# The MLP of the last 1224 tokens by seven products of halves instead of eight, in two halves of tokens

## The chip, the cores and the metric

The kernel runs on one core of one Trainium2 chip. Its engines are TensorE (PE; PEld is its weight load), VectorE (DVE), ScalarE (ACT), GpSimd (POOL) and SyncE (SP, which issues the transfers). The metric is the device time of one execution in microseconds (us), lower is better.

## The reference, cut to what matters

One decoder layer over 2048 prompt tokens and 8 new tokens, 2056 in all, with 1024 features. The part that changes is the MLP, all in float32:

```python
def _mlp(h, g, w_up, w_down):          # w_up (1024, 4096), w_down (4096, 1024)
    a = jax.nn.relu(rmsnorm(h, g) @ w_up)
    return (a * a) @ w_down
...
hp = hp + _mixer_out(outs, lses, pooled, w_out[i])
hp = hp + _mlp(hp, norm_mlp_g[i], w_up[i], w_down[i])
hp = hp + _ple(hp, p_prompt[i], ple_norm_g[i], w_ple_gate[i], w_ple[i])
```

`_ple` is a gate, `(p @ w_ple) * sigmoid(rmsnorm(h) @ w_ple_gate)`; a last RMSNorm follows.

## The kernel before

Activations lie transposed, features on the 128 partitions and tokens in the columns. Every float32 operand of a product is kept as two parts, the value rounded to fp32r and the rest of it, and a product is three matmuls (`PASSES`: high by high, high by low, low by high), so that one 128x128 weight tile by one chunk of tokens costs three matmuls into one bank of PSUM. `load_w` loads a weight tile, makes its high part on POOL (`pcopy`, L199) and its low part on DVE (a subtraction by `tt`, L196).

From the MLP on, the tokens go in two parts: X, the first 832 (chunks `CX`, two of 416), and Y, the last 1224 (chunks `CY`: 416, 416 and 392). In time: input projection and attention; MLP of X (attention of the later heads runs beside it); output projection of Y; gate of X; MLP of Y (about 1720 to 2570 us); gate of Y with the final norm. The change is in the MLP of Y, called MLP-Y below, and in what stands at its borders.

`mlp` walks 4096 hidden features in 8 blocks of 512. A block has an up side (four groups j of 128 hidden features, 24 matmuls a chunk, then relu on ACT at L1344, square on POOL, the high part on ACT at L1347, the low part on DVE) and a down side (8 output tiles `ft` times 3 chunks, 12 matmuls each, added from PSUM to the accumulator `hacc` by DVE). MLP-Y has 8 x (4 x 3 x 24 + 8 x 3 x 12) = 4608 matmuls. Each weight is loaded once for the 1224 tokens.

The program is written in the order above with generators that lay other work beside it (`Pace`, `hook`); a scheduler then sets the order on each engine, and each engine runs its own queue in that order, waiting on semaphores. `R` and `F` are two regions of on-chip memory for operands in two parts (`mem_r`) and plain float32 (`mem_f`; `mem_ma` and `mem_mb` are pieces that pass from one to the other). `tt(eng, out, a, b, op)` is an element-wise operation of two tensors on DVE (`V`) or POOL (`G`).

Of the kernel before, what the change touches and what calls it, by code (L numbers as in the profile page):

```python
# [17 lines left out]
P = 128  # L18
# [19 lines left out]
CY = [(2 * LC, LC), (3 * LC, LC), (4 * LC, T - 4 * LC)]  # L38
NX, NY = 2 * LC, T - 2 * LC

# [8 lines left out]
class Arena:  # L49
# [15 lines left out]
    def alloc(self, cols, keys=None, high=False):  # L65
# [7 lines left out]
        s = max(fits, key=lambda s: s[1]) if high else min(fits, key=lambda s: (s[3], s[2]))  # L73
# [75 lines left out]
def decoder_step(ctx: ExitStack, tc: tile.TileContext, I, O):  # L149
# [103 lines left out]
    qkvS = DR([3, NS, H * E], "qkvs_s")  # L253
    s0S = DR([2, NS * H], "s0_s")
# [97 lines left out]
    class Acts:  # L352
# [824 lines left out]
    class Stat:  # L1177


        def __init__(self, chunks, tp, eng=V):  # L1180
# [4 lines left out]
            self.sq = Ring(F, 2, LC)  # L1185
# [8 lines left out]
        def finish(self, ci):  # L1194
            ln, a, ps = self.chunks[ci][1], self.acc[ci], self.tp()
            q = ln // 4
            for i in range(4):
                mm(ps[:q, i : i + 1], a[:, i * q : i * q + q], ones[:, :1], True, True)
            v, s1, s2, r = (TINY(4, q, key="st", n=8, width=4) for _ in range(4))
            V.tensor_scalar(v, ps[:q, :4], 1.0 / D, EPS, op0=ALU.mult, op1=ALU.add)  # L1200
            newton(r, v, s1, s2)
            ps = self.tp()
            for i in range(4):
# [185 lines left out]

    def load_acc(src, chunks):  # L1390
# [6 lines left out]
    def gate(xa, hacc, sums, cis, getw, hook, step=None):  # L1397


        base, s0 = xa.chunks[0][0], xa.chunks[cis[0]][0]  # L1400
        sr, pr = Ring(F, 2, LC), Ring(F, 2, LC)
        for ft in range(KD):
            w = getw(ft)
            for ci in cis:
# [11 lines left out]
                hc = hacc[ft].ap[:, c0 - base : c0 - base + ln]  # L1416
# [7 lines left out]
                else:  # L1424
                    S.activation(hc, hc, AF.Copy, scale=g_fin[:, ft : ft + 1])
                if step:
                    step(ft, s)
# [6 lines left out]
    class Final:  # L1434


        def __init__(self, hacc, base, sums, p0, p1):
            self.hacc, self.base, self.sums, self.p0, self.tiles = hacc, base, sums, p0, []
# [5 lines left out]
        def add_up(self, ps, src, start, stop):  # L1444
            order = range(len(self.tiles))
            for i in order if start(0) else reversed(order):
# [17 lines left out]
        def turn(self, i, ft, ps):  # L1464
            p, rw = self.tiles[i]
            PE.transpose(ps[:rw, (ft % 4) * P : (ft % 4) * P + P], self.hacc[ft].ap[:, p - self.base : p - self.base + rw], ident)  # L1466
# [14 lines left out]
    def final(hacc, base, sums, p0, p1, yr):  # L1481
        fin, ps = Final(hacc, base, sums, p0, p1), tp()
# [164 lines left out]
    for b in (rr, xg):  # L1647
        b.free()
# [59 lines left out]
```

## Time and profile before

| what | value |
|---|---|
| time, median of 2 runs | 2735.38 us (2733.13 to 2737.62) |
| the profiled execution: its time, its span | 2732.91 us, 2731.2 us |
| mean granted TensorE clock, in parts of full speed | 0.991 |
| PE busy | 2651.1 us, 97% |
| DVE, POOL, ACT busy | 1559.9, 1030.2, 846.6 us (57, 38, 31%) |

The span runs from the first instruction to the last. Busy shares are means over stages with different limits, so the stage of MLP-Y has to be read by itself. A line number can be that of a helper: L190 is every matmul, L196 every element-wise operation of two tensors, and the tiles and shapes tell which is meant.

### The profile page before, as it was taken

The page shows a single profiled execution, that of the slowest core. Times are in us where ns is not written, and L with a number is a line of the kernel's source. Part 1 is how long each engine was busy: PE and PEld are TensorE (multiplying, and loading weights), DVE is VectorE, ACT ScalarE, POOL GpSimd, SP SyncE. Part 2 cuts the span into 40 slices and gives each one's busy share as a digit, 9 for nine tenths or more (in the row PEclk, how much of TensorE's full clock was granted, in tenths as well). Part 3 has the DMA queues.
Part 4 walks back from the last instruction along what each step waited for, and adds up shares of the span by engine and source line. Part 5 has one row for each costly group of instructions (what it writes and reads, how often), then busy time and mean ns, then how long its engine had stood idle before and what let it go on. Part 6 is the DMA issues. An engine that isn't in the chain of part 4 may idle for free. (4 is left out here: it accounts for less than half of the span.)

```text
span 2731.2 us, 43094 instructions
## 1 busy us (share of the span) xinstructions
PE 2651.1 (97%) x15686; PEld 2526.3 (92%) x15686; DVE 1559.9 (57%) x3373; ACT 846.6 (31%) x1605; POOL 1030.2 (38%) x1370
## 2 busy tenths in 40 slices
PE   8999999998999999999999898999999999999998
PEld 6888899978988999999999898999999999999997
DVE  6747867675587776775765857432332332332675
ACT  6221445463434134243343424301001011011354
POOL 2415745434385444343344626312112122122263
PEclk9999999999999999999999999999999999999999
DMA  7464345476154233342322545331111111111134
GB/s 248 133 180 124 86 121 136 110 224 177 49 150 113 81 88 82 97 107 71 99 73 66 167 142 149 127 104 39 42 41 42 39 39 39 39 39 39 53 84 150
DMA packets 386194, 272.51 MB, mean 100 GB/s; under 512 B 91722, under 2 KB 349461, under 8 KB 385973
## 3 DMA queue, kind: packets, MB, share of 16 engines
q1 hardware_dynamic: 385397, 269.68, 34.6%
q8 instruction: 123, 2.02, 0.3%
q14 instruction: 90, 0.74, 0.1%
q0 software_dynamic: 512, 0.07, 0.0%
q10 hardware_dynamic: 72, 0.02, 0.0%
HBM read 209.47 MB, written 60.30 MB: 99 GB/s over the span
## 5 line engine op out<-in xcount | busy, mean ns | idle before, releaser
L190 PE MATMUL bank<-mem_r 128*128 128x416 f32 (+11 forms) x13608 | 2454.0, 338 | 46.9 <-DVE mem_r L196 13.3
L190 PEld LDWEIGHTS bank<-mem_r 128*128 128x128 f32 (+2 forms) x13608 | 2307.9, 184 | 127.4 <-DVE mem_r L196 22.9
L199 POOL TENSOR_SCALAR mem_r<-mem_f 128x512 fp32r<-128x512 f32 (+1 forms) x444 | 325.2, 737 | 773.6 <-PE bank L190 689.1
L196 DVE TENSOR_TENSOR mem_r<-mem_f,mem_r 128x512 fp32r<-128x512 f32 (+3 forms) x568 | 435.5, 773 | 176.2 <-POOL mem_r L199 142.8
L196 DVE TENSOR_TENSOR mem_f<-bank,mem_f 128x416 f32<-128x416 f32 (+3 forms) x488 | 272.7, 566 | 234.5 <-PE bank L190 227.6
L196 DVE TENSOR_TENSOR mem_r<-mem_mb,mem_r 128x416 fp32r<-128x416 f32 (+6 forms) x236 | 174.0, 744 | 349.3 <-ACT mem_r L1347 318.3
L1344 ACT ACTIVATE mem_mb<-bank 128x392 f32<-128x392 f32 (+1 forms) x160 | 82.2, 514 | 801.0 <-PE bank L190 801.0
L196 POOL TENSOR_TENSOR mem_mb<-mem_mb 128x416 f32<-128x416 f32 (+1 forms) x140 | 143.7, 1027 | 304.2 <-ACT mem_mb L1344 277.9
L776 DVE CUSTOM_DVE_ANT_0 bank<-bank,mask 128x256 f32<-128x256 f32 (+3 forms) x504 | 159.8, 338 | 33.9 <-PE bank L190 30.1
L199 POOL TENSOR_SCALAR mem_r<-mem_r 128x256 fp32r<-128x256 f32 (+1 forms) x117 | 92.0, 798 | 92.2 <-PE bank L190 81.1
L196 DVE TENSOR_TENSOR mem_ma<-bank,mem_ma 128x416 f32<-128x416 f32 (+2 forms) x104 | 63.4, 610 | 87.5 <-PE bank L190 72.8
L1347 ACT CAST mem_r<-mem_mb 128x416 fp32r<-128x416 f32 (+1 forms) x128 | 68.5, 535 | 134.4 <-POOL mem_mb L196 134.4
L859 POOL TENSOR_SCALAR_AFFINE_SELECT mem_ma<-mem_ma 128x256 f32<-128x256 f32 (+2 forms) x148 | 72.0, 506 | 92.2 <-ACT mem_ma L871 49.3
L190 PE MATMUL bank<-mem_mb,mem_r 128*64 128x64 f32 (+4 forms) x494 | 100.7, 321 | 6.2 <-DVE mem_r L196 2.1
L190 PEld LDWEIGHTS bank<-mem_mb,mem_r 128*128 128x128 f32 (+1 forms) x494 | 78.7, 174 | 16.0 <-POOL mem_r L199 2.8
L196 DVE TENSOR_TENSOR mem_r<-mem_ma,mem_r 128x512 fp32r<-128x512 f32 (+4 forms) x88 | 71.6, 819 | 26.4 <-ACT mem_r L880 20.5
L199 POOL TENSOR_SCALAR mem_r<-mem_mb 128x512 fp32r<-128x512 f32 (+3 forms) x61 | 55.3, 913 | 79.4 <-PE bank L190 55.8
L196 POOL TENSOR_TENSOR mem_f<-mem_f 128x416 f32<-128x416 f32 (+2 forms) x52 | 70.0, 1351 | 31.3 <-DMA mem_f<-in_cache_attn_kv_dram 11.4
L776 DVE DVE_READ_ACCUMULATOR2_ANT mem_ma<- 128x1 f32 (+1 forms) x512 | 68.5, 134 | 0.0
L196 POOL TENSOR_TENSOR mem_ma<-mem_ma 128x416 f32<-128x416 f32 (+1 forms) x41 | 51.8, 1272 | 39.7 <-DMA mem_ma<-h_s 14.1
L196 DVE TENSOR_TENSOR mem_f<-mem_f,mem_ma 128x416 f32<-128x416 f32 (+1 forms) x64 | 46.9, 733 | 26.2 <-ACT mem_ma L1190 11.3
L859 POOL TENSOR_SCALAR_AFFINE_SELECT mem_mb<-mem_mb 128x256 f32<-128x256 f32 (+2 forms) x76 | 34.5, 474 | 57.9 <-ACT mem_mb L868 22.8
(255 smaller groups left out, 1807.7 us busy)
## 6 DMA issues: line engine op xcount, KB each, us to landing
mem_f<-in_w_up_dram SPq DMA_DIRECT2D x128, 256.0 KB
mem_f<-in_w_down_dram SPq DMA_DIRECT2D x128, 256.0 KB
mem_f<-in_w_in_dram SPq DMA_DIRECT2D x64, 256.0 KB
out_dram<-mem_f SPq DMA_DIRECT2D x55, 256.0 KB
mem_f<-in_cache_attn_kv_dram SPq DMA_DIRECT2D x48, 256.0 KB
mem_f<-in_w_ple_gate_dram SPq DMA_DIRECT2D x48, 256.0 KB
mem_f<-in_x_prompt_dram SPq DMA_DIRECT2D x64, 128.0 KB
xT_s<-mem_f SPq DMA_DIRECT2D x32, 256.0 KB
```

The source lines that it names most:

```text
L190: PE.matmul(out, l, r, start=start, stop=stop)
L196: eng.tensor_tensor(out, a, b, op=op)
L199: G.tensor_scalar(out, src, 1.0, 1.0, op0=ALU.mult, op1=ALU.mult)
L776: V.tensor_tensor_reduce(src, src, mask, 1.0, -3e38, ALU.add, ALU.max, mcol[: src.shape[0], col : col + 1])
L859: G.affine_select(out=p, in_=p, pattern=[[0, nblk], [sign, w]], compare_op=ALU.is_ge, fill=0.0, base=base, channel_multiplier=-sign)
L1344: S.activation(a, ps[:, :ln], AF.Relu)
L1347: S.copy(x[:, 0], sq)
```

## The change

MLP-Y works in two halves of 612 tokens, each two chunks of 306 (`HY`; `CY` is now four chunks of 306). In each half, tokens, inner features and outer features of a product are split in two, and the 2x2 block product is made of seven products instead of eight (`SEVEN`, Winograd's form of Strassen's), each of half size. For that, sums of blocks are formed ahead: of the weights by four additions or subtractions of 256 columns on POOL (`w_sums`), of the activations by four of 306 columns (`z_sums`). A weight of four blocks becomes seven slots: four as loaded (1024 columns) and three sums (768 columns); an activation becomes seven slots of 306 columns. All seven are split into high part (ACT) and low part (DVE), in `parts` and `z_parts`. The products meet in three banks (`b` 0, 1, 2), which are read out after certain products (`p`) and go on accumulating.

A block of 512 hidden features in a half has four steps of 84 matmuls: two up steps (j = 0, 1) and two down steps (o = 0, 2). `Fill` prepares the weights of one step (two `Weights7`) while the step before runs. Both halves load and prepare all weights. X's hidden state goes through DRAM (`hxS`) and its final norm is made from there; the first half of Y goes through `h2`.

```diff
-CY = [(2 * LC, LC), (3 * LC, LC), (4 * LC, T - 4 * LC)]
+HY = NY // 4
+CY = [(NX + i * HY, HY) for i in range(4)]
...
+    SEVEN = ((0, 0, 0, 1), (3, 3, 2, 5), (1, 1, 1, 2), (5, 5, 0, 6), (6, 2, 2, 3), (4, 4, 0, 7), (2, 6, 0, 4))
+    OPENS = (1, 2, 5)
+    def w_sums(raw, s):
+        tt(G, s[:, 0], raw[:, 0], raw[:, 3], ALU.subtract)
+        tt(G, raw[:, 3], raw[:, 3], raw[:, 2], ALU.add)
+        tt(G, s[:, 1], raw[:, 3], raw[:, 0], ALU.subtract)
+        tt(G, s[:, 2], raw[:, 1], s[:, 1], ALU.subtract)
+    def z_sums(z, eng):
+        tt(eng[0], z[:, 4], z[:, 2], z[:, 3], ALU.subtract)
+        tt(eng[1], z[:, 3], z[:, 3], z[:, 0], ALU.subtract)
+        tt(eng[2], z[:, 5], z[:, 2], z[:, 3], ALU.subtract)
+        tt(eng[3], z[:, 6], z[:, 1], z[:, 5], ALU.subtract)
+    def z_parts(dst, z):
+        for a, b in ((0, 3), (3, 7)):
+            S.copy(dst[:, 0, a:b], z[:, a:b])
+            tt(V, dst[:, 1, a:b], z[:, a:b], f(dst[:, 0, a:b]), ALU.subtract)
...
+        def parts(self, three):
+            src, ring = (self.b, self.w3) if three else (self.a, self.w4)
+            w = [x.rearrange("p (s n) -> p s n", s=3 if three else 4) for x in ring()]
+            S.copy(w[0], src)
+            tt(V, w[1], src, f(w[0]), ALU.subtract)
...
+    def prep_seven(src, rs, gc, xs, pair, zr):
...
+            for t in range(2):
+                zt = z[:, 2 * t : 2 * t + 2]
+                tt(G, zt, zt, rb[t].ap.unsqueeze(1).to_broadcast([P, 2, ln]), ALU.mult)
...
+            z_sums(z, (V, V, V, V))
...
+            z_parts(z_parts_view(x.ap), z)
...
+    def mlp_seven(xs, get_acc, rings, zr, fill, before_last, done):
+        ln = HY
+        bsets = [[bank[0], bank[1], bank[3]], [bank[4], bank[5], bank[6]]]
...
+                for slot_w, slot_z, b, p in SEVEN:
+                    products(bs, slot_w, slot_z, b, p, ws, x)
+                    ps = bs[b][:, :ln]
+                    if p in (1, 5, 6, 4):
+                        S.copy(z[:, {1: 0, 5: 2, 6: 3, 4: 1}[p]], ps)
+                    else:
+                        i = {2: 0, 3: 3, 7: 2}[p]
+                        tt(V, z[:, i], ps, z[:, i], ALU.add)
+                    if p == 7:
+                        fill.late()
+                S.activation(z[:, 0:4], z[:, 0:4], AF.Relu)
+                tt(G, z[:, 0:4], z[:, 0:4], z[:, 0:4], ALU.mult)
+                z_sums(z, (G, G, V, V))
+                r = R.alloc(14 * ln, ("r",))
+                rl.append(r)
+                z_parts(z_parts_view(r.ap), z)
...
+            for o in (0, 2):
+                pair = fill.take()
+                for slot_w, slot_z, b, p in SEVEN:
+                    for u in range(2):
+                        bs = bsets[u]
+                        products(bs, slot_w, slot_z, b, p, [pair[u]], zs)
...
+                        if p == 2 or p == 4:
+                            t = zr[1](ln)
+                            S.copy(t, bs[b][:, :ln])
+                            tt(G, hc, hc, t, ALU.add)
+                        else:
+                            tt(V, hc, bs[b][:, :ln], hc, ALU.add)
...
-    mlp(xm, get_acc_y, 512, wr, Pace(bg, 7, 24 * NY * 3.5), before_last_y)
+    hy, st1 = mlp_seven(xs, acc_of(h1, slice(y0, y1)), rings, (zring, scratch), fill, last_1, keep_1)
...
+    hy2, st2 = mlp_seven(cur["xs"], acc_of(h1, slice(y1, T)), rings, (zring, scratch), fill, last_2, lambda *_: None)
```

How the queues stand now, at two places. POOL in the middle of MLP-Y, before, where a row of 512 columns is the high part of a weight and the others square an activation:

```order
L199 TENSOR_SCALAR mem_r<-mem_f 128x512 x8
L196 TENSOR_TENSOR mem_mb_15973<-mem_mb_15973 128x416 x2
L199 TENSOR_SCALAR mem_r<-mem_f 128x512 x2
L196 TENSOR_TENSOR mem_mb_15973<-mem_mb_15973 128x392
L196 TENSOR_TENSOR mem_mb_15973<-mem_mb_15973 128x416 x2
```

One block holds 16 of the first kind and 12 squares. Now, at the end of the up side of a block; 256 columns are sums of weights, 306 sums of activations, 1224 the square of one up step:

```order
L197 TENSOR_TENSOR mem_f<-mem_f 128x256 x10
L197 TENSOR_TENSOR mem_ma_1833<-mem_ma_1833 128x1224
L197 TENSOR_TENSOR mem_ma_1833<-mem_ma_1833 128x306
L197 TENSOR_TENSOR mem_f<-mem_f 128x256
L197 TENSOR_TENSOR mem_ma_1833<-mem_ma_1833 128x306
L197 TENSOR_TENSOR mem_f<-mem_f 128x256 x4
L197 TENSOR_TENSOR mem_f<-mem_f 128x1224
L197 TENSOR_TENSOR mem_f<-mem_f 128x256 x2
```

The single-input copies of weights are gone from POOL, and in their place stand 32 sums of 256 columns a block, with the squares queued between them.

PE, before, where the up side of a block (24 in a row) gives way to the down side (12 in a row):

```order
L190 MATMUL bank_71<-mem_r 128x416 x24
L190 MATMUL bank_73<-mem_r 128x416 x24
L190 MATMUL bank_70<-mem_r 128x392 x24
L190 MATMUL bank_71<-mem_r 128x416 x12
L190 MATMUL bank_73<-mem_r 128x416 x12
```

Now, at the same place of a block (bank_74 is the first bank of the second up step, j = 1; from bank_70, single, the down side begins):

```order
L1493 MATMUL bank_74<-mem_r,mem_mb_14529 128x306 x2
L1493 MATMUL bank_74<-mem_r 128x306
L1493 MATMUL bank_70<-mem_r 128x306
L1493 MATMUL bank_71<-mem_r 128x306
L1493 MATMUL bank_75<-mem_r 128x306
L1493 MATMUL bank_70<-mem_r 128x306 x2
L1493 MATMUL bank_71<-mem_r 128x306 x2
L1493 MATMUL bank_75<-mem_r 128x306 x2
L1493 MATMUL bank_74<-mem_r 128x306 x3
```

The two products that end the second up step (p = 7 and 4 in `SEVEN`, one bank) now run straight into the down side. Of that, 18 matmuls on the result of j = 0 come first (twelve of them in these rows, six more in two other banks), and then those on the result of j = 1; before, the first products of the down side needed a chunk that had left PE two chunks earlier.

## Rows read from the trace of the kernel before

**Rows 1.** The page, part 1: busy us (share of the span) x instructions.

```profile
PE 2651.1 (97%) x15686; PEld 2526.3 (92%) x15686; DVE 1559.9 (57%) x3373; ACT 846.6 (31%) x1605; POOL 1030.2 (38%) x1370
```

**Rows 2.** Windows of 100 us: window, length, busy us, granted clock, DMA share, GB/s.

```profile
1700.00:1800.00 100.00, 98.29 (x538) 96.48 (x537) 45.97 (x69) 34.91 (x64) 37.27 (x41) 0.97 0.44 138
1900.00:2000.00 100.00, 100.00 (x541) 99.27 (x541) 30.51 (x50) 10.98 (x21) 19.97 (x25) 1.00 0.14 41
2400.00:2500.00 100.00, 100.00 (x542) 99.32 (x542) 31.09 (x50) 10.96 (x21) 20.60 (x27) 1.00 0.13 38
2500.00:2600.00 100.00, 99.96 (x550) 98.54 (x549) 55.65 (x96) 30.88 (x59) 30.64 (x33) 1.00 0.15 47
```

**Rows 3.** Timeline of PE: start, us, what, columns, count.

```profile
619.34 3.76 PE L190 MATMUL bank<-mem_r 128*128 128x256 f32 x30
...
1999.80 15.36 PE L190 MATMUL bank<-mem_r 128*128 128x416 f32 x82
```

**Rows 4.** Groups by line and shape, PE: busy us, mean ns | idle before.

```profile
L190 PE MATMUL bank<-mem_r 128*128 128x416 f32 x7584 | 1516.4, 354 | 19.3 <-DVE mem_f L196 9.3 <-DVE mem_r L196 4.2 <-ACT mem_ma L1410 2.3
...
L190 PE MATMUL bank<-mem_r 128*128 128x256 f32 x468 | 96.2, 293 | 5.8 <-POOL mem_r L199 5.3 <-DMA mem_r<-mneg 0.3 <-DVE mem_ma L776 0.2
```

**Rows 5.** The same groups of other engines, from 1750 to 2500 us.

```profile
L196 DVE TENSOR_TENSOR mem_r<-mem_f,mem_r 128x512 fp32r<-128x512 f32 x114 | 79.4, 697 | 60.4 <-POOL mem_r L199 59.4
...
L196 DVE TENSOR_TENSOR mem_f<-bank,mem_f 128x416 f32<-128x416 f32 x70 | 41.4, 592 | 106.6 <-PE bank L190 106.6
...
L1347 ACT CAST mem_r<-mem_mb 128x416 fp32r<-128x416 f32 x55 | 29.7, 540 | 53.5 <-POOL mem_mb L196 53.5
L1344 ACT ACTIVATE mem_mb<-bank 128x416 f32<-128x416 f32 x55 | 28.5, 518 | 503.8 <-PE bank L190 503.8
```

**Rows 6.** Timeline of POOL, at three places where DVE leaves it alone.

```profile
822.30 1.28 POOL L196 TENSOR_TENSOR mem_f<-mem_f 128x512 f32<-128x512 f32 x1
...
1661.84 1.08 POOL L196 TENSOR_TENSOR mem_ma<-mem_ma 128x416 f32<-128x416 f32 x1 [1.90 <-DMA mem_ma<-h_s]
...
2001.98 0.88 POOL L196 TENSOR_TENSOR mem_mb<-mem_mb 128x416 f32<-128x416 f32 x1 [3.65 <-ACT mem_mb L1344]
```

**Rows 7.** Timeline of all engines from 2614 us (gate of Y).

```profile
2614.43 1.41 POOL L196 TENSOR_TENSOR mem_mb<-mem_f,mem_mb 128x416 f32<-128x416 f32 x1
2614.83 1.47 DVE L196 TENSOR_TENSOR mem_mb<-mem_mb 128x416 f32<-128x416 f32 x1
...
2615.81 1.38 POOL L196 TENSOR_TENSOR mem_f<-mem_mb,mem_f 128x392 f32<-128x392 f32 x1
2616.22 1.42 DVE L196 TENSOR_TENSOR mem_ma<-mem_ma,mem_mb 128x416 f32<-128x416 f32 x1
...
2617.15 1.39 POOL L196 TENSOR_TENSOR mem_f<-mem_ma,mem_f 128x392 f32<-128x392 f32 x1
2617.56 1.40 DVE L1229 SCALAR_TENSOR_TENSOR mem_r<-mem_ma,gcols,mem_r 128x392 fp32r<-128x392 f32 x1
...
2618.50 0.94 POOL L199 TENSOR_SCALAR mem_r<-mem_f 128x512 fp32r<-128x512 f32 x1
```

**Rows 8.** Windows around a wait of PE: columns as in rows 2.

```profile
1516.00:1519.00 3.00, 1.24 (x6) 0.88 (x6) 3.00 (x3) 1.53 (x3) 3.00 (x3) 1.00 0.78 201
1519.00:1526.00 7.00, 5.81 (x17) 5.55 (x18) 7.00 (x10) 2.65 (x6) 7.00 (x7) 0.51 0.90 218
```

**Rows 9.** Timeline of PE there; in brackets the idle time before.

```profile
1520.19 7.01 PE L190 MATMUL bank<-mem_r 128*128 128x416 f32 x22 [2.95 <-DVE mem_f L196]
```

**Rows 10.** Timeline of SP: issues of transfers.

```profile
8.83 1.44 SPq L187 DMA_DIRECT2D mem_f<-in_x_prompt_dram  x3
...
2005.03 2.18 SPq L187 DMA_DIRECT2D mem_f<-in_w_down_dram  x2
```

More of the change, by code (lines that the diff above doesn't have):

```diff
@@ new lines, in decoder_step, with __init__, early, late @@
+    class Fill:
+        def __init__(self, steps, rings, hook):
+            self.steps, self.rings, self.hook, self.ready, self.open = iter(steps), rings, hook, [], None
+            self.early()
+            self.late()
+        def early(self):
+            step = next(self.steps, None)
+            if step is None:
+                return
+            ws = [Weights7(self.rings) for _ in step]
+            for w, at in zip(ws, step):
+                w.load(*at)
+                w.sums()
+                w.parts(False)
+            self.open = ws
+        def late(self):
+            if self.open is None:
+                return
+            for w in self.open:
+                w.parts(True)
+            self.ready.append(self.open)
+            self.open = None
+        def take(self):
+            ws = self.ready.pop(0)
+            self.early()
+            return ws
+        def work(self, n):
+            if self.hook:
+                self.hook(n)
@@ L1395, in load_acc, with gate @@
         return acc
-    def gate(xa, hacc, sums, cis, getw, hook, step=None):
-        base, s0 = xa.chunks[0][0], xa.chunks[cis[0]][0]
-        sr, pr = Ring(F, 2, LC), Ring(F, 2, LC)
+    def gate(xa, where, sums, cis, getw, hook, step=None, dump=None):
+        s0 = xa.chunks[cis[0]][0]
+        width = max(xa.chunks[ci][1] for ci in cis)
+        sr, pr = Ring(F, 2, width), Ring(F, 2, width)
         for ft in range(KD):
@@ L1444, in add_up @@
         def add_up(self, ps, src, start, stop):
[L1445 to L1446 removed]
+            order = sorted(range(len(self.tiles)), key=lambda i: -self.tiles[i][1])
+            self.widest = order[0]
+            for i in order if start(order[0]) else reversed(order):
                 p, rw = self.tiles[i]
@@ L1520, in step @@
                     fin.give(full, dh, b[1 - dh], yr())
-        gate(xa, hacc, sums, (ci,), getw, Pace(bg, nbg, 24 * ln * (KD - 3)), step)
+        gate(xa, where, sums, (ci,), getw, Pace(bg, nbg, 24 * ln * (KD - 3)), step)
     xa = [Acts(IN_PART[0], keys=("ma", "mb", "r"), high=True), Acts(IN_PART[1])]
@@ new lines, in decoder_step @@
+    zr = Ring(F, 1, 7 * HY)
+    xs = []
+    bg = prep_seven(h1, rst, g_mlp, xs, CY[:2], zr)
+    gate(xg, lambda ft, ci: hx[ft].ap[:, ci * LC : ci * LC + LC], stx.buf.ap, (0, 1), gate_w(wr), Pace(bg, 4, 24 * NX * 7), dump=hxS)
+    drain(bg)
+    finx, ps = Final(None, None, 0, NX), tp()
+    finx.add_up(ps, stx.buf.ap, lambda i: True, lambda i: True)
+    finx.rstd(ps)
+    for b in (*hx, stx.buf, xg, zr, wr):
+        b.free()
+    wp = [R.alloc(1024, ("mb",)) for _ in range(3)] + [R.alloc(n, ("r",), low=True) for n in (1024, 768, 768, 768, 768)]
@@ L1678, in decoder_step @@
+    gate(xg, where, sums.ap, (0, 1), gate_w(wr), Pace(bg, 16, 24 * 2 * HY * 7))
+    drain(bg)
+    st2.free_acc()
     tp, mp = Turns(bank[2:]), Turns(bank[:2])
```

266 lines of the change are left out of this document (211 added, 55 removed).

## The prediction

> **What bounds the kernel now.** I read the page's shares first: PE is busy 97% of the span, DVE 57%, POOL 38% [rows 1]. Then the windows of 100 us, since a share is a mean over stages: in MLP-Y, PE is busy all the time, DVE 31% and POOL 20%, and 541 or 542 matmuls pass in 100 us [rows 2]. So MLP-Y takes 4608 / 541.5 x 100 = 851 us, PE alone sets it, and the other engines have room. A change that takes matmuls away and gives DVE and POOL work is worth what PE saves, as long as the two stay below PE. That is the question here, so I looked next for what their operations cost alone [rows 5, 6] and together [rows 7].
>
> **What PE saves.** The timeline gives 82 matmuls of 416 columns in 15.36 us, of which the last lasts 0.354: 15.01 / 81 = 0.185 us each; 30 of 256 columns in 3.76, the last 0.293: 0.120 us each [rows 3, 4]. The line between them puts 306 columns at 0.120 + 50/160 x 0.065 = 0.140. The order of the changed kernel holds 16 blocks (8 in each half) of 4 x 84 = 336 such matmuls, 5376 in all: 47.1 us a block, 753 us. PE saves 98 us of 851 if nothing holds it up. Output projection and gate of Y now have 768 matmuls of 306 columns each in place of 576 of 416 and 392 (0.185 by the count above): 107.7 for 106.4 us, so about 3 us more for the two.
>
> **What DVE and POOL alone cost, per block.** POOL takes 1.28 us for a sum of two tensors of 512 columns and 1.08 for 416 [rows 6]: 2.08 ns a column, so 0.75 for 256, 0.85 for 306. A square of 416 takes 0.88 [rows 6]; with the same fixed part (0.21) 1.6 ns a column, so 2.2 for 1224. A block has 4 steps x 2 weights x 4 = 32 sums of 256 (24.0 us), 12 operations of 306 (two in each up step, four in each down step: 10.2) and two squares (4.3): 38.5 us. (A block before, 107 us for all 1224 tokens, kept POOL busy a fifth of that [rows 2].)
>
> DVE takes 0.697 for a subtraction of 512 columns with both inputs on chip and 0.592 for 416 with one input in PSUM [rows 5]; alone, both lie on one line of 1.09 ns a column. So 1024 columns cost 1.26, 768 0.98, 306 0.47, 918 1.14, 1224 1.47. Operations with both inputs outside PSUM: 8 weights x 2.24 = 17.9; four sums of 306 = 1.9; two times 918 and 1224 = 5.2; together 24 operations, 25.0 us. Additions from PSUM: 3 in each up step, 10 in each down step, 26 x 0.47 = 12.3. DVE 37.3 us in all.
>
> ACT: three groups of 416 columns cost 0.54 each [rows 5], so by columns at most 8 x 1792 (weights) + 2 x 4590 (up steps) + 8 x 306 (down steps), 26,000 columns a block at 1.3 ns, 34 us. Each engine alone lies below PE's 47.1. SP issues 8 transfers a step; a transfer costs it 0.48 to 1.09 us [rows 10], so at most 8.7 us of a step of 11.8. The weights are loaded twice: the DMA share of 0.13 at 38 to 41 GB/s [rows 2] doubles, which is far from full. I cost both at nothing; cover for them is the step ahead in which they run.
>
> **What DVE and POOL cost together.** At 2614 us both have work queued, on operands that do not concern each other. POOL's operations, 1.08 alone at 416 columns, take 1.38 to 1.41; DVE's, 0.59 alone, take 1.40 to 1.47, and their ends alternate: DVE about 0.46 us after POOL, POOL 0.9 after DVE [rows 7]. They take turns, and the time of an operation holds its wait for the turn. POOL starts at 2614.43, 2615.81, 2617.15 and 2618.50: 1.36 us for a pair that alone costs (1.67 + 1.62 + 1.62) / 3 = 1.63. So a DVE operation with two inputs outside PSUM and a POOL operation exclude each other but for about 0.27 us of a pair. The additions from PSUM keep 592 ns as the mean of 70, some beside POOL's work [rows 5], so I count them free of it.
>
> Then POOL and the two-input work of DVE must fit one after the other: 38.5 + 25.0 - 24 x 0.27 = **57.0 us a block**, 10 more than PE needs. Sixteen blocks: 912 us. This is the term on which the forecast rests. PE will wait for parts of weights and activations; POOL will hardly wait. The end of the up side (the order above) adds a wait for PE: read-out of j = 1, relu, square, high part, of which the square alone is 2.2 us and the three ACT operations between 1.6 us (as at 416 columns) and 3.3 (by columns), 3.8 to 5.5, behind 18 matmuls = 2.5 us. That is 1.3 to 3.0 us a block on PE, inside the 10 us that it has to spare, so I charge nothing for it.
>
> **The borders.** Work beside the last block of each half comes on top, since the same two engines set the pace there. Preparing the second half of Y: 4 steps of two POOL operations of 612 columns (1.49 each) and six on DVE (4 x 0.47 + 1.14 + 1.47): 4 x (2.98 + 4.49 - 6 x 0.27) = 23 us. The gate's normalization: 12 POOL operations of 306, 4 on DVE, 16 two-input splits on DVE at about 0.5: 10.2 + 1.9 + 8 - 20 x 0.27 = 15. Sums of squares, 28 x (0.47 - 0.27) = 6. Together 44 us, at most; the one step whose successor is not prepared gives some 8 back, and POOL's own waits at the ends of up sides take about as much, so I let these two cancel.
>
> **The sum.** MLP-Y 912 + 44 = 956 for 851: +105. Gate and projection: +3. The profiled execution took 2732.9 us: 2841. The median shown is 2.5 above it: **2843 us**.
>
> **Bounds, and a page against them.** The dearest unknown is the sum of 256 columns, which no row shows. From below: in proportion to columns, 1.28 / 2 = 0.64 and 0.76 for 306, POOL 33.9, a block 52.4. From above, 0.85 as for 306 gives 60. The Trainium skill, page "GPSIMD Engine Reference", section "Performance versus the Vector engine", gives 4497 ns for an addition of 2048 columns on GpSimd; in proportion (an estimate from that page) 0.56 for 256 columns, a block of about 49, and a sum near 2710. The trace does not agree at 512 columns, 1.28 where that proportion gives 1.12 [rows 6], so I keep the line through the rows.
>
> **Rivals.**
> *PE stays the bound (faster).* If DVE and POOL do not exclude each other with these longer operands, the longest engine is PE with 47.1 and its 1.3 to 3.0 of wait: 16 x 49 = 784 us, borders hidden: 2735 - 67 + 3 = 2671. For it: every engine alone is below PE. Against it: [rows 7], three pairs in a row. It decides from a block below about 50 us with hidden borders. 0.08.
> *The pair binds, but cheaper (within 2%).* POOL's operations in proportion to columns, 52.4 a block, and borders half hidden: 838 + 25 = 863, +12 and the 3 of gate and projection: about 2750. Everything from 2681 to 2790 belongs here. For it: the fixed part of a POOL operation is extrapolated from two rows. 0.22.
> *Waits add up (slower still).* When PE waits at the end of an up side, its next window can run at the lower level: after 2.95 us of waiting the granted clock is 0.51 of full (1.2 for 2.4 GHz) in the 7 us that follow [rows 8, 9], which costs some 3.4 us of matmuls, and DVE's additions, queued behind a split that itself waits for POOL, hold the banks. If these waits are not covered by POOL's backlog, a block is 57 + 3 + 3 = 63: 1008 + 44, +204: about 2940. 0.12.
> *The change does not do what it says*: excluded, the order holds 5376 matmuls of 306 columns and 512 sums of 256 on POOL.
>
> **How the numbers follow.** Forecast (2790 to 2900) 0.58, and the rivals as above. The range leaves out PE as the bound and the far end of the added waits: 2750 to 2930. A measurement of this kernel can tell about 2%, 55 us, from no change; slower by more than that is the forecast and the third rival, 0.70; within, 0.22; faster, 0.08.
>
> **What would show it.** In windows over the new MLP-Y: POOL and DVE both busy (with their waits) above 85%, PE below 88%, and the matmuls of 306 at 0.14 us where they run freely. In the groups: sums of 256 columns on POOL alone near 0.75 and on the mean above 1.0; DVE's 1024 above its 1.26. In the waits of PE: DVE and ACT, behind whom POOL stands. A block should last 55 to 60 us, 16 times. Wrong would be: PE above 95% busy there (the first rival), sums of 256 near 0.6 (the second), or POOL idle for more than a tenth of the stage, which would mean that a chain of waits and not the two engines' work sets the block.

## The result, and the profile after

The changed kernel takes **3043.52 us** (median of 2 runs, 3042.65 to 3044.38) where the kernel before takes 2735.38: 1.113 times as long, with a 95% interval of 1.108 to 1.117. The profiled execution took 3044.38 us, its span 3042.7. The forecast was 2843 us, slower by 108; it is slower by 308.

The page's part 1 of the changed kernel answers to [rows 1]: PE's share fell from 97 to 89%, and nobody took its place. POOL is busy 56% and DVE 67% of the span.

```profile
PE 2709.8 (89%) x16858; PEld 2545.9 (84%) x16858; DVE 2047.0 (67%) x3870; ACT 1215.8 (40%) x2102; POOL 1694.4 (56%) x1915
```

Windows of the changed kernel: the first and second answer to [rows 2] (columns as there), the third is three blocks of the first half, from the relu that begins the chain of one block to that of the third block after it.

```profile
1900.00:2000.00 100.00, 81.65 (x513) 78.55 (x512) 63.14 (x70) 43.11 (x61) 77.14 (x70) 0.92 0.23 66
2400.00:2500.00 100.00, 83.53 (x538) 80.43 (x537) 61.57 (x73) 42.16 (x60) 76.76 (x71) 0.93 0.23 67
...
1989.20:2190.40 201.20, 162.56 (x1008) 156.08 (x1008) 130.54 (x151) 83.29 (x116) 154.46 (x139) 0.89 0.22 64
```

A block lasts 201.20 / 3 = **67.1 us**. PE is busy 54.2 us of it, POOL 51.5, DVE 43.5, ACT 27.8. None of them is busy all the time: this is the line to see. PE was busy 100 of 100 us in this stage before; now it is idle for 12.9 us of a block, and the granted clock is 0.89 on the mean where it was 1.00.

The difference to the forecast, on the profiled executions (3044.4 against 2841), has three parts. Sixteen blocks at 67.1 and not 57.0 are 162 us. The products of MLP-Y run from 1751.7 to 2888.0 us, 1136.3, of which the sixteen blocks are 1073.6: 63 us for the borders, where 44 were forecast, 19 more. The rest of the kernel takes 3042.7 - 1136.3 = 1906.4 us, 26.2 more than before (2731.2 - 851 = 1880.2), where 3 were forecast: 23 more. So four fifths of the miss lie in the length of a block, and the experiments are about that.

The groups of the changed kernel from 1900 to 2700 us (busy us, mean ns | idle before) answer to [rows 4 to 6].

```profile
L1493 PE MATMUL bank<-mem_r 128*128 128x306 f32 x2928 | 512.2, 327 | 117.0 <-DVE mem_r L197 66.2 <-ACT mem_f L1510 24.3 <-ACT mem_r L1417 22.5
...
L197 POOL TENSOR_TENSOR mem_f<-mem_f 128x256 f32<-128x256 f32 x368 | 379.2, 1048 | 157.4 <-DVE mem_r L197 151.1 <-DMA mem_f<-in_w_down_dram 1.6
...
L197 DVE TENSOR_TENSOR mem_r<-mem_f,mem_r 128x768 fp32r<-128x768 f32 x92 | 122.0, 1326 | 36.0 <-ACT mem_r L1444 36.0
...
L197 DVE TENSOR_TENSOR mem_f<-bank,mem_f 128x306 f32<-128x306 f32 x190 | 84.6, 467 | 61.2 <-PE bank L1493 61.2
...
L197 DVE TENSOR_TENSOR mem_r<-mem_ma,mem_r 128x1224 fp32r<-128x1224 f32 x15 | 45.2, 3016 | 15.8 <-ACT mem_r L1417 15.8
...
L197 POOL TENSOR_TENSOR mem_ma<-mem_ma 128x1224 f32<-128x1224 f32 x11 | 24.5, 2228 | 0.0
...
L197 DVE TENSOR_TENSOR mem_r<-mem_f,mem_r 128x1224 fp32r<-128x1224 f32 x11 | 15.8, 1433 | 14.7 <-ACT mem_r L1417 14.7
```

The prices of single operations came out as forecast: the additions from PSUM 0.467 (forecast 0.47), the square of 1224 columns 2.23 (2.2), the sums of 256 columns on the mean above 1.0, with 0.74 for the one at 1983.95 below, which starts before the split beside it (0.75). What was not forecast stands behind the last bar of POOL's sums: 151.1 us in which POOL waited for DVE to split an earlier set of sums and so free the buffer. And DVE's low part of an activation takes 1.43 us on the mean in one buffer (mem_f, the second up step) and 3.0 in the other (mem_ma, mostly the first). POOL's wait goes back to PE, as the timeline from 1981 us shows: the sum waits for a split on DVE, the split for a cast on ACT, and the cast for PE to give its buffer back.

```profile
1982.05 1.68 ACT L1444 CAST mem_r<-mem_f 128x768 fp32r<-128x768 f32 x2 [0.90 <-PE bank L1493]
1982.91 0.96 DVE L197 TENSOR_TENSOR mem_r<-mem_f,mem_r 128x768 fp32r<-128x768 f32 x1 [1.07 <-ACT mem_r L1444]
...
1983.95 0.74 POOL L197 TENSOR_TENSOR mem_f<-mem_f 128x256 f32<-128x256 f32 x1 [5.27 <-DVE mem_r L197]
```

How the waits come about is seen in the timeline of all engines in one passage from the up to the down side, from 1984 to 2012 us of the changed kernel.

```profile
1983.95 8.40 POOL L197 TENSOR_TENSOR mem_f<-mem_f 128x256 f32<-128x256 f32 x8 [5.27 <-DVE mem_r L197]
...
1986.69 1.05 ACT L1444 CAST mem_r<-mem_f 128x1024 fp32r<-128x1024 f32 x1 [2.97 <-PE bank L1493]
...
1988.22 1.05 ACT L1444 CAST mem_r<-mem_f 128x1024 fp32r<-128x1024 f32 x1 [0.16 <-POOL mem_f L197]
1989.17 1.22 ACT L1516 ACTIVATE mem_ma<-mem_ma 128x1224 f32<-128x1224 f32 x1
...
1990.30 0.39 ACT L1510 COPY mem_f<-bank 128x306 f32<-128x306 f32 x1
...
1990.75 1.95 PE L1493 MATMUL bank<-mem_r 128*128 128x306 f32 x12 [2.01 <-ACT mem_f L1510]
...
1992.31 3.63 POOL L197 TENSOR_TENSOR mem_ma<-mem_ma 128x1224 f32<-128x1224 f32 x2
1992.67 2.68 DVE L197 TENSOR_TENSOR mem_r<-mem_f,mem_r 128x768 fp32r<-128x768 f32 x1 [1.34 <-ACT mem_r L1444]
...
1995.28 0.46 DVE L197 TENSOR_TENSOR mem_f<-bank,mem_f 128x306 f32<-128x306 f32 x1
...
1995.80 1.74 PE L1493 MATMUL bank<-mem_r,mem_mb 128*128 128x306 f32 x8 [3.10 <-DVE mem_f L197]
...
1998.86 12.92 POOL L197 TENSOR_TENSOR mem_f<-mem_f 128x256 f32<-128x256 f32 x10
...
1999.04 1.23 ACT L1516 ACTIVATE mem_f<-mem_f 128x1224 f32<-128x1224 f32 x1
...
2002.06 1.99 ACT L1444 CAST mem_mb<-mem_f 128x1024 fp32r<-128x1024 f32 x2
2002.19 3.42 DVE L197 TENSOR_TENSOR mem_r<-mem_ma,mem_r 128x1224 fp32r<-128x1224 f32 x1 [1.33 <-ACT mem_r L1417]
...
2002.21 0.55 PE L1493 MATMUL bank<-mem_r 128*128 128x306 f32 x2 [1.22 <-ACT mem_r L1417]
...
2005.53 1.75 DVE L197 TENSOR_TENSOR mem_mb<-mem_f,mem_mb 128x1024 fp32r<-128x1024 f32 x1
...
2005.67 2.41 PE L1493 MATMUL bank<-mem_r 128*128 128x306 f32 x8 [2.91 <-DVE mem_r L197]
2007.20 1.75 DVE L197 TENSOR_TENSOR mem_r<-mem_f,mem_mb 128x1024 fp32r<-128x1024 f32 x1
2008.88 1.63 DVE L197 TENSOR_TENSOR mem_r<-mem_f,mem_r 128x918 fp32r<-128x918 f32 x1
2010.57 1.64 PE L1493 MATMUL bank<-mem_r 128*128 128x306 f32 x5 [2.49 <-DVE mem_r L197]
```

Follow PE's waits from line to line. The one of 2.01 us ends with ACT's read-out of a bank at 1990.30; in ACT's queue that read-out stands behind two casts of weights, of which the first waited 2.97 us, and behind the relu. The one of 3.10 us ends with DVE's addition at 1995.28, which stands behind a split of 768 columns; that split lasts 2.68 us and not 0.96 as at 1982.91, because POOL's square runs at the same time. The one of 2.91 us ends with the low part of 1224 columns, 3.42 us long beside POOL's sums. The one of 2.49 us ends with the low part of 918 columns, which stands behind two splits of weights of 1.75 us each. The square itself (1992.31) had to wait for the eight sums of weights ahead of it on POOL. It belongs to the first up step (mem_ma), and so do the high and the low part for which PE waits 1.22 and 2.91 us: not only the second up step comes late. So work for the next step stands in three queues ahead of the work that PE waits for, and takes turns with it.

The granted clock in the windows of the same passage (columns as in rows 2) shows the second half of the price.

```profile
1988.70:1995.80 7.10, 1.99 (x14) 1.70 (x13) 5.73 (x6) 4.61 (x6) 6.94 (x5) 1.00 0.51 148
1996.70:2000.10 3.40, 3.40 (x15) 3.40 (x14) 2.75 (x4) 1.48 (x2) 3.40 (x4) 0.51 0.00 0
2003.50:2013.70 10.20, 5.54 (x20) 5.16 (x21) 8.64 (x8) 2.42 (x4) 8.99 (x7) 0.50 0.35 103
2014.00:2026.00 12.00, 12.00 (x87) 12.00 (x86) 8.64 (x14) 3.87 (x6) 5.76 (x6) 1.00 0.01 2
```

After two waits with 1.99 us of work in 7.10, the clock is granted at the lower of its levels (1.2 for 2.4 GHz): by the records, the matmuls that start from 1996.82 to 1999.88 us are 0.255 us apart, where those from 2014 to 2026 us, at the full clock, are 0.141 apart.

### The profile page after: what moved, and what is told of

Same layout as the page of the kernel before. It is cut to its first block, busy times and chain, and to the rows that moved or that the text cites. A ratio compares the mean times of both kernels' runs of the same rounds, so it can differ in the third digit from the quotient of the medians.

```text
span 3042.7 us, 48726 instructions
## 1 busy us (share of the span) xinstructions
PE 2709.8 (89%) x16858; PEld 2545.9 (84%) x16858; DVE 2047.0 (67%) x3870; ACT 1215.8 (40%) x2102; POOL 1694.4 (56%) x1915
## 4 chain that ended last, share of the span: by engine, by line
POOL 15%; issue 15%; DVE 9%; PE 6%; DMA 5%; ACT 2%; SPq 0%; POOLq 0%; DVEq 0%; ACTq 0%
POOL mem_f L197 11%; PE bank L191 5%; DVE mem_r L197 4%; POOL mem_ma L197 4%; DVE mem_ma L197 2%; DVE mem_f L197 1%; DVE mem_mb L197 1%; DVE mem_r L1235 1%; PE bank L1493 1%; DMA mem_f<-ple_s 1%; DMA mem_ma<-h_s 1%; ACT mem_r L1417 1%; POOL mem_r L200 1%; DMA mem_f<-in_w_ple_gate_dram 0%; SPq L188 0%
## 5 line engine op out<-in xcount | busy, mean ns | idle before, releaser
L191 PE MATMUL bank<-mem_r 128*128 128x416 f32 (+9 forms) x9384 | 1612.0, 328 | 56.9 <-DVE mem_r L197 14.9
L191 PEld LDWEIGHTS bank<-mem_r 128*128 128x128 f32 (+1 forms) x9384 | 1476.2, 184 | 131.4 <-DVE mem_r L197 25.1
L197 POOL TENSOR_TENSOR mem_f<-mem_f 128x256 f32<-128x256 f32 (+4 forms) x739 | 806.0, 1116 | 278.7 <-DVE mem_r L197 198.6
L1493 PE MATMUL bank<-mem_r 128*128 128x306 f32 x4096 | 724.0, 329 | 164.1 <-DVE mem_r L197 91.5
L197 DVE TENSOR_TENSOR mem_r<-mem_f,mem_r 128x512 fp32r<-128x512 f32 (+7 forms) x682 | 669.3, 987 | 232.1 <-ACT mem_r L1444 96.6
L1493 PEld LDWEIGHTS bank<-mem_r 128*128 128x128 f32 x4096 | 659.0, 208 | 196.6 <-DVE mem_r L197 108.1
L197 DVE TENSOR_TENSOR mem_f<-bank,mem_f 128x416 f32<-128x416 f32 (+5 forms) x640 | 324.3, 521 | 190.1 <-PE bank L191 98.6
L1493 PE MATMUL bank<-mem_r,mem_mb 128*128 128x306 f32 x1280 | 250.5, 329 | 57.1 <-DVE mem_f L197 42.1
L1493 PEld LDWEIGHTS bank<-mem_r,mem_mb 128*128 128x128 f32 x1280 | 214.3, 209 | 67.6 <-DVE mem_f L197 47.4
L197 DVE TENSOR_TENSOR mem_r<-mem_ma,mem_r 128x512 fp32r<-128x512 f32 (+5 forms) x142 | 174.5, 1235 | 47.4 <-ACT mem_r L1417 22.8
L197 DVE TENSOR_TENSOR mem_ma<-bank,mem_ma 128x306 f32<-128x306 f32 (+1 forms) x208 | 103.4, 503 | 109.5 <-DMA mem_ma<-xT_s 41.1
L197 POOL TENSOR_TENSOR mem_ma<-mem_ma 128x306 f32<-128x306 f32 (+2 forms) x73 | 107.9, 1479 | 25.6 <-DMA mem_ma<-h_s 13.1
```

Source lines behind the costliest of these rows:

```text
L191: PE.matmul(out, l, r, start=start, stop=stop)
L197: eng.tensor_tensor(out, a, b, op=op)
L1493: PE.matmul(banks[b][:, :ln], ws[k // 2].at(slot_w, i, k % 2), z[:, j, slot_z], start=n == 0 and p == OPENS[b], stop=n == last, skip_group ...
```

## The experiments

Of every run I took three blocks in the middle of the first half, from relu to relu. "Neither" is worked out from the records of these blocks: the time in which no POOL operation and no DVE operation without an operand in PSUM is under way. Each run is one execution; the kernel before took 2731.6 to 2740.0 us on the same chips. The scheduler orders the queues anew for every program: ACT's order over a block is that of the changed kernel in e1_nolow and nearly that in e12_nosplit, and another one in the other runs, so there the worth of an edit includes that of another order.

| kernel | time, us | block, us | PE busy | clock | POOL busy | neither |
|---|---|---|---|---|---|---|
| changed | 3043.5 | 67.1 | 54.2 | 0.89 | 51.5 | 11.2 |
| e1_nolow (control) | 3038.6 | 66.8 | 54.8 | 0.87 | 51.6 | 10.9 |
| e2b_sets_late | 3066.0 | 69.4 | 56.6 | 0.86 | 47.8 | 13.2 |
| e2_sets | 3064.2 | 69.4 | 56.8 | 0.85 | 47.9 | 13.1 |
| e3_nosums | 2947.6 | 61.5 | 53.6 | 0.92 | 19.3 | 25.7 |
| e5_nosquare | 2980.9 | 63.3 | 53.8 | 0.91 | 41.0 | 12.8 |
| e8_spare | 3080.6 | 70.3 | 61.8 | 0.93 | 49.6 | 13.9 |
| e11_narrow | 3010.6 | 64.5 | 51.1 | 0.83 | 51.9 | 9.2 |
| e12_nosplit | 2924.1 | 59.1 | 52.1 | 0.94 | 40.8 | 17.4 |
| e6_pipe | 2950.2 | 62.5 | 52.7 | 0.93 | 51.5 | 7.5 |
| e7_pipe_nosums | 2789.0 | 50.5 | 48.9 | 1.00 | 18.2 | 14.3 |
| e9_pipe_sets | 2936.6 | 59.5 | 51.5 | 0.97 | 53.0 | 4.6 |
| e10_pipe_nosplit | 2776.6 | 49.4 | 47.8 | 1.00 | 41.1 | 7.9 |

In the changed kernel POOL and that part of DVE together are under way for 67.1 - 11.2 = 55.9 us of a block. The forecast's sum for the pair was 57.0. So the theories are: **the pair** (its work sets the block, whatever waits), **the loop of buffers** (POOL's wait for the buffer of the sums), and **the chain** (queues at the end of the up side make PE wait, and each wait brings a stretch of lower clock).

### e1_nolow: the control

It reads the high part of the MLP's input in place of its low part on the up side, and so frees memory for others.

```diff
-            x = R.alloc(14 * ln, ("r",), low=True)
+            x = R.alloc(7 * ln, ("r",), low=True)
...
-        x = [z_parts_view(b.ap) for b in xs]
+        x = [High(z_view(b.ap)) for b in xs]
```

> Leaves out the low part of the MLP's input in its second half-set: the up products read the high part in its place (as many matmuls as before), which frees 8568 columns of memory and drops 8 splits on VectorE at the borders. It is the control for the run with more buffers. Both theories (the pair: VectorE and GpSimd exclude each other and so set 57 of the 67 us of a block; the loop: one set of buffers for the sums makes GpSimd wait for VectorE's splits of the sums before, which wait for TensorE) expect nearly no change, 3020 to 3045 us, and a block of 66 to 68 us.

Measured 3038.6, 5 us less, with the same block within 0.3 us. What is built on it can be compared with the changed kernel.

### e2b_sets_late and e2_sets: more buffers for the sums

Both have twice the buffers for the three sums and for their parts, and one more for loaded weights. e2b also makes the parts of the sums at once.

```diff
-    w3 = Turns([wa[4:6], wa[6:8]])
+    w3 = Turns([wa[4:6], wa[6:8], wa[8:10], wa[10:12]])
...
 (e2b alone)
                 w.parts(False)
+                w.parts(True)
```

> The control, with twice the buffers for the sums of weights (four for float32 sums, four pairs for their parts, four for loaded weights), and the parts of the sums made as soon as the sums are there. The loop: GpSimd no longer waits for VectorE's splits, its idle 15 us a block go, a block falls from 67 to 57 to 60 us, the time to 2870 to 2930. The pair alone: GpSimd and VectorE have the same work and the same exclusion, block 64 to 67, time above 2990. A third theory, that the chain at the end of an up side (read-out, relu, square, high part) sets the block: no change, above 3010.

> The control without low parts of the MLP's input (3038.6, block 66.8 us) with twice the buffers for the weight sums, for their parts and one more for loaded weights; unlike the earlier run with these buffers (3066.0) the parts of the sums are still made late, where the changed kernel makes them, so the buffers are the only edit. If POOL's waits for a buffer (12.9 us a block) set the block: it falls to 58 to 62, the kernel 2890 to 2960. If PE's waits at the end of the up side set it, where POOL's sums stand in one queue with the square and ACT's weight casts in one with relu: 65 to 69, the kernel 3010 to 3070, as POOL's waits only move.

3066.0 and 3064.2: a block of 69.4 us, 2.6 more than the control. POOL no longer waits for the buffer, but neither-time rose to 13.1. The wait only moved: in e2_sets POOL now waits 10.5 us a block for ACT's read-outs and 7.9 for the relu, by the records. ACT's order changed with it: the relu of the first up step starts 3.6 us before that of the second, where it was 10 us in the changed kernel. So more buffers do not shorten the block in the order that came with them, and the loop of buffers as the only cause is not borne out, here or in e3 below; the buffers with the old order were not run.

### e3_nosums and e5_nosquare: less work for POOL

e3 leaves the sums of the weights out (the slots hold loaded blocks), e5 leaves out the square and moves its step's two sums of activations from POOL to DVE.

```diff
 (e3)
-                w.sums()
 (e5)
-                tt(G, z[:, 0:4], z[:, 0:4], z[:, 0:4], ALU.mult)
-                z_sums(z, (G, G, V, V))
+                z_sums(z, (V, V, V, V))
```

> Leaves out the 512 sums of weights on GpSimd: the slots of sums hold loaded blocks instead. All splits and all matmuls stay. The pair: 24 us a block less on GpSimd, its work and VectorE's two-input work one after the other 36 us, so TensorE with its waits is the bound, a block of 49 to 53, time 2750 to 2830. The loop: the same, since 10 us of each step's chain go. The chain at the end of an up side: that chain stays, a block of 58 or more, time above 2890.

> Leaves out the square of the activation on GpSimd and moves the two sums of activations there to VectorE: GpSimd has 7.7 us a block less, VectorE 1.9 more. The pair: 5 to 6 us a block less, time 2940 to 2960. The loop: the sums of weights wait as before, at most 2 us a block, 3010 to 3040. The chain at the end of an up side: 2.2 us and GpSimd's queue leave it, twice a block, 4 to 9 us a block, 2900 to 2980.

2947.6 and 2980.9. e3 takes 32 us of POOL's busy time out of a block, and the block becomes 5.6 us shorter; POOL is then busy 19.3 of 61.5 us. If the pair set the block, it would have come to PE's own time. e5 takes away 10 us of POOL and gets 3.8; its time lies 1 us above what the chain was given and 21 above the pair's range. In both, PE goes on waiting for ACT's high parts and read-outs and for DVE's low parts.

### e6_pipe and e7_pipe_nosums: the two sides interleaved

Built on the control: an up step of the next block stands ahead of each pair of down products, so that the down side reads activations that were made a step or more ago. e7 leaves the sums of weights out as well.

```diff
+        for _ in range(2):
+            up(acts[0])
...
             for o in (0, 2):
+                if not last:
+                    up(acts[blk + 1])
...
+                down(o, zs, last)
```

> Built on the control without low parts of the MLP's input (the products of the up side read the high part in place of the low one), which took 3038.6 with a block of 67 us; this frees the memory that two more sets of activations need. Changed beside it: the two up products of the next block are issued one ahead of each down pair of the block before it, so that no down product waits for activations that have just been made. Theory A (the chain at the end of the up side: read-outs, relu, square, sums, parts, with the weight sums of POOL in the same stretch, makes PE wait 12.7 us a block, and each wait is followed by some us at half the clock, which cost 7 more): the waits fall below 4 us and the half clock below 6 us a block, block 50 to 58 us, the kernel 2790 to 2920. Theory B (POOL and DVE together need 67 us a block wherever the work stands, the waits only show it): block 64 to 68 us with the waits moved elsewhere, the kernel 2995 to 3055. In between (the pair's own sum of the prediction, 57 us, binds once the chain is gone): 56 to 60 us, PE waits of 5 to 9 us spread over the block and POOL busy over 85%.

> As the run with the two sides interleaved, and without the four sums of the weights on POOL (the sum slots hold loaded blocks, so the products are not Strassen's). Without the interleaving this took 2947.6 with a block of 61 us. Theory A: with both the chain and the weight sums gone PE is all that is left, block 47 to 52 us, the kernel 2740 to 2820. If the interleaving alone gives as much (within 15 us of it), POOL and DVE do not bind in it; if this one is 60 us or more faster, they still do. Theory B: 2920 to 2950, as without the interleaving.

2950.2: theory A's range was missed by 30 us on one side, theory B's by 45 on the other. The case between them was missed too, with a block of 62.5 and not 56 to 60. PE's waits are 9.8 us, and POOL is busy 51.5 us (82%) and waits 5.9 for a buffer. e7, 2789.0, is theory A's: 50.5 us, clock 1.00. The rows of three blocks each, e6 first.

```profile
1938.80:2126.30 187.50, 157.96 (x1008) 151.76 (x1008) 128.83 (x150) 82.27 (x116) 154.56 (x139) 0.93 0.23 68
```

```profile
1919.40:2070.90 151.50, 146.61 (x1011) 142.80 (x1010) 110.50 (x150) 81.04 (x116) 54.74 (x42) 1.00 0.29 84
```

With the sides interleaved the same removal of the sums is worth 12.0 us a block (62.5 to 50.5) where it was worth 5.6. So there are two limits close to each other, and I had both theories too simple: take one away and the other stands a few us below.

### e8_spare and e11_narrow: is PE itself in the loop?

e8 gives PE 74 unneeded matmuls in ten blocks where it waits, into a bank that nobody reads. e11 computes 256 of the 306 columns of each product.

```diff
 (e8)
+                    if j == 1 and p in (7, 4):
+                        spare(blk, 14 if p == 7 else 20, ws, x)
...
+            spare(blk, 40, ws, x)
 (e11)
-                    PE.matmul(banks[b][:, :ln], ws[k // 2].at(slot_w, i, k % 2), z[:, j, slot_z],
+                    PE.matmul(banks[b][:, :256], ws[k // 2].at(slot_w, i, k % 2), z[:, j, slot_z][:, :256],
```

> The changed kernel, with 74 matmuls more in ten of its sixteen blocks (the second to the sixth full block of each half), which read a first block of weights and of input into a bank that nobody reads and stand where PE waits at the end of the up side: 10.4 us of PE's time at 0.140 us each against 12.7 us of waits. If the half clock behind the waits costs the 7 us a block that theory A charges, PE that works through them stays at the full clock and the block with more work is shorter: 60 to 64 us in place of 67, the kernel 2985 to 3015. If the half clock costs nothing because the chain on ACT, DVE and POOL sets the pace anyway, the block stays at 66 to 69, the kernel 3035 to 3070.

> The changed kernel with products of 256 columns in place of 306 (the last 50 columns of each product are not computed; ACT, DVE and POOL work on all 306 as before). PE's own work falls from 47.1 to 40.3 us a block (0.120 for 0.140 us a matmul), 6.8 us less, 109 us in sixteen blocks. If PE stands in the loop that sets the block (its products lie between one read-out and the next, and its slow stretches count), the block falls by 4 to 7 us, to 60 to 63, the kernel 2935 to 2985. If the loop runs through POOL, DVE and ACT alone and PE's low clock and its work are hidden in it, the block falls by less than 2.5 us, the kernel 3005 to 3045, and PE's waits grow by what its work loses.

Both missed the range that charged the clock in full; e8 lies 10 us above the other one, too. In e8 the clock is better (0.93) and PE's idle time falls from 12.9 to 8.5 us; of the 10.4 us of spare work, 3.2 lengthen the block. But ACT's queue changed with the edit. In the changed kernel the second relu (1999.04 above) starts right behind the read-out that it needs, ahead of the casts into mem_mb. In e8 one of these casts stands ahead of it and waits for POOL's sums, so that the relu starts 3.6 us after its read-out, in each of the ten blocks and in no other:

```profile
2010.35 0.41 ACT L1517 COPY mem_f<-bank 128x306 f32<-128x306 f32 x1
2013.40 1.05 ACT L1444 CAST mem_mb<-mem_f 128x1024 fp32r<-128x1024 f32 x1 [2.64 <-POOL mem_f L197]
2014.35 1.22 ACT L1523 ACTIVATE mem_f<-mem_f 128x1224 f32<-128x1224 f32 x1
```

That delay is as long as the lengthening, so e8 does not show what the clock is worth. In e11 PE has 6.8 us less to do at the full clock, but its clock falls to 0.83 and its busy time by only 3.1; the block is 2.6 us shorter, at the edge of the "hidden" case (less than 2.5), the kernel, 3010.6, inside its range, and PE's idle time is 13.4. About 40% of the saving arrives, and the lower clock takes back about half; here, too, ACT's order is another. I can't say from these two how many of the 6.4 us that the lower clock adds to PE's busy time (54.2, against 47.8 in e10 at a clock of 1.00) lengthen the block.

### e9_pipe_sets: interleaved, and more buffers

Twice the buffers for the sums and one more for loaded weights; for the memory the down side reads the activations' high part in place of the low one, which DVE still makes.

```diff
-    wf = Ring.of([F.alloc(1024, ("f",)) for _ in range(3)]), Ring.of([F.alloc(768, ("f",)) for _ in range(2)])
+    wf = Ring.of([F.alloc(1024, ("f",)) for _ in range(3)] + [F.alloc(1024, ("mb",))]), Ring.of([F.alloc(768, ("f",)) for _ in range(2)] + [F.alloc(768, ("mb",)) for _ in range(2)])
```

> The interleaved kernel (2950.2, block 62.5 us: 55.0 in which POOL or a two-input operation of DVE on on-chip memory works, 7.5 in which neither does, 5.9 of it POOL waiting for a buffer of weight sums to be split) with twice the buffers for the three sums (four of 768 columns) and one more for loaded weights. For the memory the down products read the high part of the activations in place of the low one, as the up side does for its input already; DVE still makes the low part, into a buffer that nobody reads. Theory: POOL and DVE together need 55 to 57 us a block, the prediction's sum, and what lies above is time in which both wait; with the buffers POOL can start the next sums at once, so neither-time falls to 1 to 4 us and the block to 56 to 60, the kernel 2850 to 2910. Rival (the waits sit in the order of the queues, the buffers do not matter): block 61 to 64, 2930 to 2975.

The block is 59.5, in the theory's range; the kernel, 2936.6, lies in the rival's, since the later blocks take 59 to 62 us and the borders more. Neither-time is 4.6 and not 1 to 4, and POOL still waits 6.2 us a block for DVE's splits (5.9 in e6); what went is its wait of 4.5 us for ACT's read-outs. Of three blocks:

```profile
1941.00:2119.60 178.60, 154.46 (x1011) 146.32 (x1010) 126.36 (x151) 81.32 (x115) 159.04 (x139) 0.97 0.25 71
```

POOL is busy 159.04 / 178.60 = 89%. The pair's time is 59.5 - 4.6 = 54.9 us, as in e6 (55.0) and in the changed kernel (55.9). Three kernels with blocks of 59.5, 62.5 and 67.1 us have the same pair time; they differ in neither-time, 4.6, 7.5 and 11.2. In these kernels, which keep all of the pair's work, the pair is the floor, and the waits are what lies on it.

### e12_nosplit and e10_pipe_nosplit: POOL left alone by DVE

The splits of the weights on DVE (1024 and 768 columns) are left out, and the products read the high part of a weight twice. POOL keeps every instruction. e12 has the changed kernel's order, e10 the interleaved one.

```diff
-            tt(V, w[1], src, f(w[0]), ALU.subtract)
+            w = [w[0], w[0]]
```

> The changed kernel, in its own order, without the splits of the weights on DVE (the products read the high part of the weights in place of the low one). POOL keeps all its work. Interleaved, the same edit took the block from 62.5 to 49.4. If the 11 us a block in which neither engine works come from the order of the up and down side alone, they stay here and POOL's part shrinks by 10 (51.5 to 41): block 56 to 60, the kernel 2870 to 2935. If most of the wait is links of the chain stretched by taking turns, it goes with them: block 49 to 54, the kernel 2760 to 2840. If turns do not matter in this order because the chain's own length sets it: 63 to 67, the kernel 2980 to 3045.

> The interleaved kernel without the splits of the weights on DVE (its two-input operations of 1024 and 768 columns, 23.0 us a block); the products read the high part of the weights in place of the low one. POOL keeps all of its work. If the two engines exclude each other (the pair), POOL's operations go back towards their time alone (39 to 42 us a block), the block falls to PE's own 49 to 53 us and the kernel to 2770 to 2840, although not one instruction of POOL was taken away. If POOL by itself or its queue sets the pace, POOL stays at 49 to 52 us busy and the block at 58 to 62, the kernel 2890 to 2950.

2924.1 with a block of 59.1, the first case of its expectation; 2776.6 with a block of 49.4, the pair's case. The windows of three blocks, e12 first, then e10:

```profile
1973.30:2150.60 177.30, 156.29 (x1010) 149.65 (x1008) 64.31 (x102) 81.84 (x116) 122.34 (x140) 0.94 0.25 72
```

```profile
1914.30:2062.40 148.10, 143.44 (x1010) 142.46 (x1010) 65.21 (x102) 80.53 (x115) 123.33 (x139) 1.00 0.30 86
```

and POOL's sums of weights in the groups of the same stretches, e6 (with splits), then e10 (without):

```profile
L197 POOL TENSOR_TENSOR mem_f<-mem_f 128x256 f32<-128x256 f32 x97 | 103.4, 1081 | 19.4 <-DVE mem_r L197 17.8
```

```profile
L197 POOL TENSOR_TENSOR mem_f<-mem_f 128x256 f32<-128x256 f32 x97 | 78.9, 831 | 12.4 <-ACT mem_r L1444 10.4
```

Not one instruction of POOL was taken away, and its busy time falls from 51.5 to 41.1 us a block, the mean sum from 1.08 to 0.83 us. That is the exclusion of [rows 7] at the new lengths. The Trainium skill, page "SBUF — State Buffer", section "SBUF: two separate sides", states it as a lock: of a GpSimd operation and a DVE operation with two inputs in SBUF, whichever starts first keeps the shared ports for the whole instruction. The records agree that the two exclude each other, by this fall of 10 us; which of them goes first no run here tests.

In the changed kernel's order, PE's waits with no splits are still 7.0 us a block and the clock 0.94, and the block 9.7 us above the interleaved one. So that order costs about 10 us even with the splits out of the way; and in the interleaved order the splits cost 13.1 (62.5 to 49.4) and the sums 12.0, although PE there no longer waits for parts of activations (its longest waits, 4.5 us a block, are for high parts of weights). Order and splits together cost 67.1 - 49.4 = 17.7.

## Why the prediction was wrong

The direction was right, and most terms of the sum held. In the order of its steps:

- **PE's saving** held. 47.1 us a block were forecast; with waits out of the way PE is busy 47.8 (e10). A matmul of 306 columns takes 0.141 us at the full clock, forecast 0.140.
- **The prices of DVE and POOL alone** held, as the groups above show, and so did the pair's sum: **57.0 us forecast, 54.9 to 55.9 measured** in three kernels. The exclusion on which it rests was shown by e10. (The rows of ACT show two groups of 416 columns, 0.52 and 0.54 us, and not three; its bound of 34 us a block held, at 27.8.)
- **The step that failed** is the sentence "PE will wait for parts of weights and activations; POOL will hardly wait", and with it the chain at the end of the up side, "inside the 10 us that it has to spare, so I charge nothing for it". POOL's queue is no backlog that always has work. Its next sums need a buffer that is free only after DVE's late split, and its square needs a relu that stands behind casts on ACT. When the chain stops PE, it stops POOL a little later. Neither engine works for 11.2 us of a block: 11.2 x 16 = 179 us charged at nothing, of a miss of 203 (the pair itself came out 1.1 us a block below its 57.0). The step also took the parts of the first up step's result as ready behind the 18 matmuls; PE waits 1.22 and 2.91 us for them. PE's spare time and the pair's were taken for the same 10 us; a wait has to fit into the slack of *both*.
- **The price of the chain** was 1.3 to 3.0 us, from its operations alone. Measured are some six waits, 12.9 us a block. The operations of the chain take turns as well (a low part 3.42 for 1.43 us, a split 2.68 for 0.96) and stand behind work for the next step, which no sum of durations shows.
- **The borders** cost 63 us, not 44, and the stages around 26, not 3; the 42 us above the forecast were not taken apart. From one half to the next the relus are 106.0 us apart, 39 more than a block; there the clock is granted at 0.50 from 2314.1 to 2351.6 us, and PE is busy for 23.4 of these 37.5 us.
- **The third rival**, waits that add up with the clock behind them, came nearest to the mechanism, at 0.12. It had the place, but its price, 3 + 3 us a block, was half of the 11 that lie on the pair. Its test, POOL idle for more than a tenth of the stage, was met at once: 15.6 of 67.1 us.
- **The low clock** is there (0.89). It adds 6.4 us to PE's busy time of a block, beside the 12.9 us in which PE stands idle. How much of the 6.4 lies on the path stays open, since e8 and e11 changed ACT's order as well. No run changed the order of the queues alone, either.

No kernel here beats the one before. The best block, 49.4 us, leaves out the splits of the weights, and the kernel still takes 2776.6: with PE's 47.8 x 16 = 765 us, the waits and the borders, its products of MLP-Y take 869 us against 851 before, and the rest of the kernel 25 us more than before, nearly as in the changed one.

## What to carry to other kernels

When two engines exclude each other, their sum is a floor and not a forecast: ask of each whether its queue always holds something that can start, and look for the operation that stands at the head of the queue and waits for a third engine. A change that moves work to engines with room also puts it into their queues, ahead of the read-outs and parts that the main engine needs next, so cost the chain from read-out to next product with everything that stands ahead of it in each queue. And undo two suspects together before calling either harmless: alone, interleaving and leaving out the splits were worth 4.6 and 8.0 us a block, together 17.7.

## What the runs showed of the hardware that I had not expected

The low clock returned in all sixteen blocks of the changed kernel: waits of 2.01 and 3.10 us with 1.95 us of matmuls between were followed by 0.51 of full in the next 3.4 us, and waits of 1.22, 2.91 and 2.49 by 0.50 over 10.2 us. In the three blocks of e10, whose waits of PE are 1.6 us a block, it was 1.00 throughout. Spare matmuls in PE's waits raised the mean clock (0.89 to 0.93 in e8); what that is worth in time, e8 does not show.
